# Wide source runs for the loads, and engine programs written without a block, in a batched matrix product

## The chip, the cores and the metric

The kernel runs on one core of a Trainium2 chip. The metric is the device time of one execution in microseconds (us), the median of several. The profiler also records one execution per kernel with a time stamp for every instruction, DMA packet and semaphore update; its length from the first to the last instruction is called the span, and it is about 2 us shorter than the reported time.

Engines are named as the profile names them: PE multiplies matrices (PEld loads its weights), DVE and ACT copy and cast, POOL is used here for semaphores only, SP issues the DMAs. A DMA is carried out by sixteen DMA engines, which each move a share of it and add 1 to its semaphore when their share has landed (48 DMAs leave 768 landings in the trace). HBM is the main memory, where x, y and the result lie; SBUF holds the tiles, in 128 partitions (rows); PSUM is where PE leaves its sums. A source run is a stretch of contiguous bytes that a DMA reads as one piece; a written row is a piece that it writes into one partition of SBUF.

## The reference

For each of 16 batches, x has 768 rows of 512 floats and y 768 rows of 1,024. The result is x transposed times y, 512 by 1,024.

```
batch, m, k, n = 16, 512, 768, 1024
np.einsum('bkm,bkn->bmn', x, y).astype(np.float32)
```

So 75.50 MB are read and 33.55 MB written. No order of work avoids them.

## The kernel before

Per batch, x is loaded as 128 partitions of 12,288 bytes and y as 128 of 24,576, both contiguous in HBM. DVE casts them to bf16, y in two halves, PE makes 48 matmuls of 128x512, ACT copies the sums from PSUM, and a store of 128 rows of 16,384 bytes writes the batch. Loads have two staging buffers each, outputs five; a store is issued four batches behind the loads.

```
LAG = 4
NO = 5
@block.sync
def _(sync):
    def store(b):
        sync.wait_ge(outs, b + 1)
        sync.dma_start(o_v[b], ob[b % NO][:]).then_inc(so[b % NO], 16)
    for b in range(B):
        i = b % 2
        if b >= 2:
            sync.wait_ge(cast, b - 1)            # both x and y of batch b-2 cast
        sync.dma_start(xs[i][:], x_v[b]).then_inc(sx[i], 16)
        sync.dma_start(ys[i][:], y_v[b]).then_inc(sy[i], 16)
        if b >= LAG:
            store(b - LAG)
    ...
@block.tensor
def _(tensor):
    with tensor.Fori(0, B // 2):
        batch(tensor, 0, False)
        batch(tensor, 1, False)
@block.scalar                                     # one copy for each 128x1024 of sums
...
```

## Time and profile before

| | before |
|---|---|
| median time, us | 262.99 (262.69 to 263.14) |
| span of the profiled execution, us | 261.2 |
| x: DMA issue to landing, us | 20.8 |
| y: DMA issue to landing, us | 27.7 |
| DMA queue's share of sixteen engines' span | 98.1% |

The last line is the one to start with. The prediction below shows the lines of the page and of the table by stage. The issues of the profile (what, engine, count, size, median us from issue to landing) show how deep the queue is:

```profile
ys<-in_y_dram SPq DMA_DIRECT2D x16, 3072.0 KB, 27.7
out_dram<-ob SPq DMA_DIRECT2D x16, 2048.0 KB, 32.1
xs<-in_x_dram SPq DMA_DIRECT2D x16, 1536.0 KB, 20.8
```

An x of 1.57 MB needs 3.7 us of moving. It lands 20.8 us after its issue because other transfers stand ahead of it.

### The profile page before, as it was taken

Reading aid. Unit: us, or ns where it says so; the run is one execution under the profiler, and the core shown is the slowest. Engines: PE = TensorE matmul, PEld = TensorE weight load, DVE = VectorE, ACT = ScalarE, POOL = GpSimd, SP = SyncE. Lnnn points to the kernel's source line nnn. Section 1 sums busy time; section 2 is a strip of 40 time slices with the busy share of each in tenths; the row PEclk is TensorE's granted clock in tenths of the full one; section 3 lists DMA queues with packets and bytes.
Section 4 is the critical chain, followed back from the end, with each engine's and each line's share of the span. In section 5 each row is a group of like instructions: output and inputs, shape, how many; then the busy total and the mean of one; then the engine's idle time right before and its main releaser. Section 6 shows DMA issues by size and latency. Waiting matters only on the chain. (4 is left out here: it accounts for less than half of the span.)

```text
span 261.2 us, 1938 instructions
## 1 busy us (share of the span) xinstructions
PE 188.0 (72%) x768; PEld 87.1 (33%) x768; DVE 83.0 (32%) x48; ACT 66.1 (25%) x65; POOL 0.2 (0%) x4
## 2 busy tenths in 40 slices
PE   0039999998948949398595997939678394896920
PEld 0014555443513515144152342514334142342500
DVE  0261734435223252322524214252132523225000
ACT  1003343433331314114032140412314033131410
POOL 0000000000000000000000000000000000000000
PEclk9999999999986999979798697997999899797995
DMA  7999999999999999999999999999999999999993
GB/s 265 431 425 427 438 411 453 425 386 418 446 420 439 420 430 446 415 441 420 439 437 412 447 423 440 415 432 442 423 434 420 435 433 423 440 433 421 434 421 141
DMA packets 6915, 109.09 MB, mean 418 GB/s; under 512 B 768, under 2 KB 768, under 8 KB 768
## 3 DMA queue, kind: packets, MB, share of 16 engines
q1 hardware_dynamic: 6912, 109.05, 98.1%
q8 instruction: 1, 0.02, 0.0%
q14 instruction: 2, 0.02, 0.0%
HBM read 75.50 MB, written 33.55 MB: 417 GB/s over the span
## 5 line engine op out<-in xcount | busy, mean ns | idle before, releaser
L105 PE MATMUL ps<-yb,xb 128*128 128x512 bf16 x768 | 188.0, 406 | 61.6 <-PEq L100 55.9
L105 PEld LDWEIGHTS ps<-yb,xb 128*128 128x128 bf16 x768 | 87.1, 116 | 162.1 <-issue 96.7
L125 ACT COPY ob<-ps 128x1024 f32<-128x1024 f32 x64 | 64.9, 1013 | 183.6 <-PE ps L105 183.6
L93 DVE CAST yb<-ys 128x3072 bf16<-128x3072 f32 x32 | 54.9, 1757 | 88.4 <-DMA ys<-in_y_dram 88.4
L89 DVE CAST xb<-xs 128x3072 bf16<-128x3072 f32 x16 | 28.2, 1760 | 67.5 <-DMA xs<-in_x_dram 66.8
L125 ACT ACT_TABLE_LOAD x1 | 1.3, 1283 | 1.0 <-SPq L44 1.0
L142 POOL MEMSET const-uint8-127<- 128x1 uint8 x1 | 0.1, 102 | 0.0
L142 POOL MEMSET const-bfloat16-1.0<- 128x1 bf16 x1 | 0.1, 101 | 0.0
L142 POOL MEMSET const-float32-0.0<- 128x1 f32 x1 | 0.1, 98 | 0.2 <-issue 0.2
L142 POOL MEMSET const-float32-1.0<- 128x1 f32 x1 | 0.1, 98 | 0.0
## 6 DMA issues: line engine op xcount, KB each, us to landing
ys<-in_y_dram SPq DMA_DIRECT2D x16, 3072.0 KB, 27.7
out_dram<-ob SPq DMA_DIRECT2D x16, 2048.0 KB, 32.1
xs<-in_x_dram SPq DMA_DIRECT2D x16, 1536.0 KB, 20.8
```

The costliest lines, as they stand in the source:

```text
L89: nc.vector.tensor_copy(xb[i][:], xs[i][:]).then_inc(ready, 1)
L93: nc.vector.tensor_copy(yb[i][:, ks], ys[i][:, ks]).then_inc(ready, 1)
L105: mm = nc.tensor.matmul(ps[mo][:, nt], x_w[:, kt, mo], yb[i][:, kt, nt * NF:(nt + 1) * NF], start=(kt == 0), stop=(kt == KT - 1))
L125: nc.scalar.copy(ob[b % NO][:, mo].rearrange("p (t f) -> p t f", f=NF), ps[mo][:]).then_inc(room, 1)
L142: nc = _bacc.Bacc("TRN2", target_bir_lowering=False, num_devices=1)
```

## The change

The intent: the block goes (the frame that the engines' programs stand in, with a barrier at its end, where the engines wait for each other); each staging buffer is given back as soon as its own cast is done; and source runs are made as long as they can be, 49,152 bytes, which span four partitions of x or two of y. The first load of x and of y stays plain and serves as a pattern for the others. Casts of y become one instruction in batches 3 to 13, copies from PSUM become half as many and twice as large, and POOL passes the casts' count to PE. The core of the diff (cut at "..."):

```
-    ps = [... nc.psum_tensor(f"ps{i}", [P, NT, NF], FP32) for i in range(MT)]
+    HB = MT // 2
+    ps = [... nc.psum_tensor(f"ps{i}", [P, HB, NT, NF], FP32) for i in range(2)]
...
-    block = ec(nc.Block())
...
+    def wide_dma(key, dst, src, dram_rows, load):
+        ...
+        widen = lambda a: a.rearrange("(q r) k m -> q (r k m)", r=dram_rows)
+        plain = lambda a: a.rearrange("p k m -> p (k m)")
+        s, d = (widen(src), plain(dst)) if load else (plain(src), widen(dst))
...
+        if b < B - 2:
+            nc.sync.wait_ge(groups, 2 * (b + 2))
+        else:
+            nc.sync.wait_ge(outs, b - (B - 3))
...
+        if b >= 2:
+            nc.sync.wait_ge(cast, nx[b - 2])
+        wide_dma("x", xs[i][:], x_v[b], 4, True).then_inc(sx[i], 16)
+        if b >= 2:
+            nc.sync.wait_ge(cast, nx[b - 2] + parts(b - 2))
+        wide_dma("y", ys[i][:], y_v[b], 2, True).then_inc(sy[i], 16)
...
+    for b in range(B):
+        nc.gpsimd.wait_ge(cast, nx[b]).then_inc(ready, 1)
...
```

More of the change, by code (lines that the diff above doesn't have):

```diff
@@ L3 @@
 _os.environ.setdefault("NEURON_RT_ULTRASERVER_MODE", "4")
+import copy as _copy
 from contextlib import ExitStack
@@ L10 @@
 from concourse._compat import with_exitstack
+from concourse.ordered_engine_set import OrderedEngineSet
 @with_exitstack
@@ L41 @@
     KH = KT // 2
-    GP = NT * NF
     ctx.enter_context(tc.tile_critical())
@@ L50 @@
     ob = [ec(nc.sbuf_tensor(f"ob{i}", [P, MT, N], FP32)) for i in range(NO)]
-    ps = [ec(nc.psum_tensor(f"ps{i}", [P, NT, NF], FP32)) for i in range(MT)]
+    HB = MT // 2
+    ps = [ec(nc.psum_tensor(f"ps{i}", [P, HB, NT, NF], FP32)) for i in range(2)]
     sx = [ec(nc.semaphore(f"sx{i}")) for i in range(2)]
@@ L59 @@
     outs = ec(nc.semaphore("outs"))
-    block = ec(nc.Block())
-    @block.sync
-    def _(sync):
-        def store(b):
-            sync.wait_ge(outs, b + 1)
-            sync.dma_start(o_v[b], ob[b % NO][:]).then_inc(so[b % NO], 16)
-        for b in range(B):
-            i = b % 2
-            if b >= 2:
-                sync.wait_ge(cast, b - 1)
-            sync.dma_start(xs[i][:], x_v[b]).then_inc(sx[i], 16)
-            sync.dma_start(ys[i][:], y_v[b]).then_inc(sy[i], 16)
-            if b >= LAG:
-                store(b - LAG)
-        for b in range(B - LAG, B):
-            store(b)
-        for i in range(NO):
-            sync.wait_ge(so[i], 16 * len(range(i, B, NO)))
@@ L81, in _ @@
-    @block.vector
-    def _(vector):
-        for b in range(B):
-            i = b % 2
-            n = 16 * (b // 2 + 1)
-            if b >= 2:
-                vector.wait_ge(groups, MT * (b - 1))
-            vector.wait_ge(sx[i], n)
-            nc.vector.tensor_copy(xb[i][:], xs[i][:]).then_inc(ready, 1)
-            vector.wait_ge(sy[i], n)
-            for h in range(2):
-                ks = slice(h * KH, (h + 1) * KH)
-                nc.vector.tensor_copy(yb[i][:, ks], ys[i][:, ks]).then_inc(ready, 1)
-            vector.drain().then_inc(cast, 1)
@@ L96, in batch @@
-    def batch(tensor, i, first):
-        x_w = xb[i][:].rearrange("p k (j mo) -> p k mo j", mo=MT)
-        tensor.wait_ge(ready, 2).then_inc(ready, -2)
-        for mo in range(MT):
-            tensor.wait_ge(room, 1).then_inc(room, -1)
-            for nt in range(NT):
-                for kt in range(KT):
-                    if mo == 0 and nt == 0 and kt == KH:
-                        tensor.wait_ge(ready, 1).then_inc(ready, -1)
-                    mm = nc.tensor.matmul(
-                        ps[mo][:, nt], x_w[:, kt, mo],
-                        yb[i][:, kt, nt * NF:(nt + 1) * NF],
-                        start=(kt == 0), stop=(kt == KT - 1))
-            mm.then_inc(groups, 1)
@@ L111, in _ @@
-    @block.tensor
-    def _(tensor):
-        with tensor.Fori(0, B // 2):
-            batch(tensor, 0, False)
-            batch(tensor, 1, False)
-    @block.scalar
-    def _(scalar):
-        nc.scalar.nop().then_inc(room, MT)
-        for b in range(B):
-            for mo in range(MT):
-                if mo == 0 and b >= NO:
-                    scalar.wait_ge(so[b % NO], 16 * (b // NO))
-                scalar.wait_ge(groups, MT * b + mo + 1)
-                nc.scalar.copy(ob[b % NO][:, mo].rearrange("p (t f) -> p t f", f=NF),
-                               ps[mo][:]).then_inc(room, 1)
-            scalar.drain().then_inc(outs, 1)
+    made = {}
@@ new lines, in wide_dma @@
+    def wide_dma(key, dst, src, dram_rows, load):
+        if key not in made:
+            made[key] = nc.sync.dma_start(dst, src)
+            return made[key]
+        pat = mybir.BassSymbolicTensorAccessPattern
+        widen = lambda a: a.rearrange("(q r) k m -> q (r k m)", r=dram_rows)
+        plain = lambda a: a.rearrange("p k m -> p (k m)")
+        s, d = (widen(src), plain(dst)) if load else (plain(src), widen(dst))
+        return nc.sync.add_instruction(_copy.replace(
+            made[key].ins, name=nc.get_next_instruction_name(),
+            ins=(pat(ap=s.ap, dtype=s.dtype, bass_ap=s, is_dma=False),),
+            outs=(pat(ap=d.ap, dtype=d.dtype, bass_ap=d, is_dma=False),),
+            sync_info=None, ant_dge_precooked=False))
@@ new lines, in parts, with store @@
+    def parts(b):
+        return 2 if b in (0, 1, 2, 14, 15) else 1
+    nx = [sum(1 + parts(a) for a in range(b)) + 1 for b in range(B)]
+    def store(b):
+        if b < B - 2:
+            nc.sync.wait_ge(groups, 2 * (b + 2))
+        else:
+            nc.sync.wait_ge(outs, b - (B - 3))
+        nc.sync.dma_start(o_v[b], ob[b % NO][:]).then_inc(so[b % NO], 16)
+    for b in range(B):
+        i = b % 2
+        if b >= 2:
[4 more added lines that the diff above has]
+        wide_dma("y", ys[i][:], y_v[b], 2, True).then_inc(sy[i], 16)
+        if b >= LAG:
+            store(b - LAG)
@@ new lines @@
+    for b in range(B - LAG, B):
+        store(b)
+    for b in range(B):
+        i = b % 2
+        n = 16 * (b // 2 + 1)
+        if b >= 2:
+            nc.vector.wait_ge(groups, 2 * (b - 1))
+        nc.vector.wait_ge(sx[i], n)
+        nc.vector.tensor_copy(xb[i][:], xs[i][:]).then_inc(cast, 1)
+        nc.vector.wait_ge(sy[i], n)
+        for h in range(parts(b)):
+            ks = slice(h * KT // parts(b), (h + 1) * KT // parts(b))
+            nc.vector.tensor_copy(yb[i][:, ks], ys[i][:, ks]).then_inc(cast, 1)
@@ new lines, with batch @@
+    for b in range(B):
+        nc.gpsimd.wait_ge(cast, nx[b]).then_inc(ready, 1)
+        for h in range(parts(b)):
+            nc.gpsimd.wait_ge(cast, nx[b] + h + 1).then_inc(ready, 2 // parts(b))
+    def batch(i):
+        x_w = xb[i][:].rearrange("p k (j mo) -> p k mo j", mo=MT)
+        nc.tensor.wait_ge(ready, 2).then_inc(ready, -2)
+        for g in range(2):
+            nc.tensor.wait_ge(room, 1).then_inc(room, -1)
+            for m in range(HB):
+                for nt in range(NT):
+                    for kt in range(KT):
+                        if g == 0 and m == 0 and nt == 0 and kt == KH:
+                            nc.tensor.wait_ge(ready, 1).then_inc(ready, -1)
+                        mm = nc.tensor.matmul(
+                            ps[g][:, m, nt], x_w[:, kt, g * HB + m],
+                            yb[i][:, kt, nt * NF:(nt + 1) * NF],
+                            start=(kt == 0), stop=(kt == KT - 1))
+            mm.then_inc(groups, 1)
@@ new lines @@
+    pe = nc.tensor.engine
+    with nc.Fori(0, B // 2, engines=OrderedEngineSet([pe])):
+        batch(0)
+        batch(1)
+    nc.scalar.nop().then_inc(room, 2)
+    for b in range(B):
+        if b >= NO:
+            nc.scalar.wait_ge(so[b % NO], 16 * (b // NO))
+        for g in range(2):
+            nc.scalar.wait_ge(groups, 2 * b + g + 1)
+            cp = nc.scalar.copy(ob[b % NO][:, g * HB:(g + 1) * HB].rearrange("p m (t f) -> p m t f", f=NF),
+                                ps[g][:])
+            if b < B - 1:
+                cp.then_inc(room, 1)
+        if b == B - 2:
+            nc.scalar.drain().then_inc(outs, 1)
@@ L131 @@
+    cp.then_inc(outs, 1)
+    for i in range(NO):
+        nc.sync.wait_ge(so[i], 16 * len(range(i, B, NO)))
 _INS = ['x', 'y']
```

## The prediction

> **What bounds the kernel now.** I read the page's busy shares first, then its DMA rows, then the busy table by stage, then the end in order of time, and last the packet and landing records of the trace.
>
> ```profile
> PE 188.0 (72%) x768; PEld 87.1 (33%) x768; DVE 83.0 (32%) x48; ACT 66.1 (25%) x65; POOL 0.2 (0%) x4
> ...
> DMA  7999999999999999999999999999999999999993
> ...
> DMA packets 6915, 109.09 MB, mean 418 GB/s; under 512 B 768, under 2 KB 768, under 8 KB 768
> ...
> q1 hardware_dynamic: 6912, 109.05, 98.1%
> ...
> L105 PE MATMUL ps<-yb,xb 128*128 128x512 bf16 x768 | 188.0, 406 | 61.6 <-PEq L100 55.9
> ...
> L93 DVE CAST yb<-ys 128x3072 bf16<-128x3072 f32 x32 | 54.9, 1757 | 88.4 <-DMA ys<-in_y_dram 88.4
> ```
>
> No compute engine is over 72%, while the queue's packets fill 98.1% of sixteen DMA engines' span. PE idles 61.6 us, most of it at the point where it waits for a batch's casts, and the casts wait 88.4 us for y to land. The chain runs from the loads to the casts to the matmuls. The table by stage (length, busy of PE, PEld, DVE, ACT, POOL, granted clock, DMA share, GB/s) says the same from start to end:
>
> ```profile
> 60.00:120.00 60.00, 45.93 (x192) 21.30 (x190) 20.76 (x12) 16.23 (x16) 0.00 (x0) 0.91 1.00 430
> 120.00:180.00 60.00, 45.87 (x174) 19.87 (x172) 19.00 (x11) 14.55 (x15) 0.00 (x0) 0.86 1.01 432
> 180.00:240.00 60.00, 44.77 (x184) 20.54 (x183) 20.76 (x12) 15.84 (x16) 0.00 (x0) 0.92 1.00 430
> 240.00:245.00 5.00, 5.00 (x24) 2.53 (x23) 0.00 (x0) 1.48 (x2) 0.00 (x0) 0.95 0.99 423
> 245.00:250.00 5.00, 4.67 (x22) 2.24 (x20) 0.00 (x0) 1.85 (x3) 0.00 (x0) 1.00 1.01 433
> 250.00:255.00 5.00, 0.00 (x0) 0.00 (x0) 0.00 (x0) 0.72 (x1) 0.00 (x0) 0.92 0.98 419
> 255.00:262.00 7.00, 0.00 (x0) 0.00 (x0) 0.00 (x0) 0.00 (x0) 0.00 (x0) 0.50 0.26 110
> ```
>
> DMA share is 1.00 in every long stage: the queue never runs dry. Only the ends are not full: the first packet starts 1.95 us into the span, and the last store is issued when the other stores are almost drained:
>
> ```profile
> 249.71 1.01 ACT L125 COPY ob<-ps 128x1024 f32<-128x1024 f32 x1 [1.58 <-PE ps L105]
> 250.78 0.33 SPq L66 DMA_DIRECT2D out_dram<-ob  x1
> ```
>
> The trace's semaphore landings show one more thing. The sixteen shares of one DMA do not land together: x of batch 0 lands over 1.16 us, and from about 38 us on the last engine is some 2.4, later 3.3 us behind the first. The one 16 KB instruction fetch in the span, a packet of 1.07 us at 38.0 us, comes just as the spread jumps from 1.17 to 2.37. The last store's shares land from 256.89 to 259.79, median 257.17; so the end is set by one laggard engine 2.6 us behind the median.
>
> **What the Trainium skill says.** "DMA: Bandwidth & Descriptors", section "Where 436 GB/s comes from", puts a ceiling of 435.2 GB/s (16 ports of 32 bytes at 850 MHz) on a core's DMA; the 430 to 432 GB/s of the stages agree and lie 1% under it. The same page, "Why small descriptors are slow (HBM only)", names a fixed overhead of about 3 cycles a packet. The packet records here have something like it, but larger: 12,288 bytes (x) take 460 ns in the median, 24,576 (y) 912 ns. The difference, 452 ns for 12,288 bytes, is 27.2 GB/s an engine, 435 over sixteen; what is left of either is **8 ns a packet**. "HBM Reference", section "Specifications (TRN2)", says a lone core is bounded by its engines at about 425 GB/s, not by the shared 358; this core ran over both figures.
>
> **The change, part by part.**
>
> Bytes do not change: 75.50 MB read, 33.55 written. At 435.2 GB/s they take 250.6 us. With the first packet at 1.95 us and 1.8 us from the last packet to the end of the span, that alone is 254.4 us of a 261.2 us span; the reported time is 1.8 us above the span (262.99 against 261.2). So no rearrangement of the same bytes can save more than about 6.8 us, 2.6%, and the bulk of these is not in reach.
>
> (a) Wide source runs. Each engine now takes 8 packets of every DMA: 16 x 8 = 128 of x and 128 of y. The landings of the fastest engine agree: y to next x 3.69 us = 8 x 460, x to y 7.30 us = 8 x 912, plus a 9 ns semaphore. If a packet is a source run, x has runs of 49,152 bytes, 2 for an engine, and y 4: 32 + 64 = 96 in place of 256 (first loads stay plain, which I neglect). 160 packets x 8 ns = **1.28 us** off each engine's queue, all of it on the path. If all 256 gaps vanished it would be 2.05 us. If the 8 ns belongs to the SBUF side, where there are still 128 rows, it is 0. Stores point to the load direction as its home: their landings step by 4.84 us, 604 ns a packet, against 602.4 at 27.2 GB/s; hardly any gap. They don't say which side. I take two thirds of 1.28: **0.85 us**.
>
> (b) Staging freed by each cast. x of batch b+2 is issued after x's cast, not after both y casts. In the first period that is about 9 us earlier (9.45 for 18.49 us). But the order in the queue stays x, y, store, and it is never empty: landing comes 20.8 (x) and 27.7 us (y) after issue. Gain **0**.
>
> (c) Own programs without the block. The block's exit is on the path: the last landing is noticed at 259.80, its barrier ends and the next stage begins at 260.18. That is up to 0.38 us; I take 0.3, and 0.05 for the entry. **0.35 us**.
>
> (d) Fewer, larger instructions. y is cast in one piece in batches 3 to 13, so PE starts a batch up to 1.76 us later; PE needs some 12 us of a period of 15.8, which leaves room. POOL relays the casts: the starting barrier's relay took 0.12 us from wait to release. Stores wait for PE having finished the next batch; that is about 3 us before the loads ahead of them can be issued. **0** in the middle.
>
> (e) The end. The last copy is 128x2048, at most twice 1.01 us, so the last store starts 1.0 us later after PE; with the relay 1.1, less the 1.4 us by which y of batch 15 would land earlier. The fast engines are through with their backlog then, and idle 1 us or so. The laggard still has over 2 us of backlog, and it sets the end: **0** if the laggard stays.
>
> Sum: 262.99 - 0.85 - 0.35 = 261.8. The spread can only be rerolled: the sides of it that I see (a 16 KB instruction fetch, first packets of 0.96 to 1.74 us) may shrink with other programs, worth up to 1.2 us. I subtract 0.2 for this: **261.6 us**.
>
> **Rivals.** *The transfer is bound by bytes, not packets*: the SBUF side sets the 8 ns, or the longer reads make the write side wait. Then (a) gives 0 and the time is 262.6. For it: 430 of 435 GB/s leaves little. Against: the gap is seen in loads and not in stores. *PE or the end becomes the bound*: if the engines level out, the last store's issue at about 250.5 us plus 5.5 us to land is the limit, span about 257.5, time 259.3; so this rival helps, and its later copy takes back up to 1 us of it. PE as the bound in the middle would need 16 x 15.8 us; it is 188 us busy. *Wide reads disturb the engines*: 48 KB runs mean that an engine stays on one region of HBM, and one stalled run delays four partitions. Nothing in the trace speaks for it; 3% lower load rate would cost 5 us (load packets are 177.5 us of each engine).
>
> **Range and chances.** Without (a) and with a worse spread 263.0; with all of the 2.05 us, the 0.35 and 0.8 of the laggard 259.9. That is my range. Faster by 2% means under 257.7: it needs the whole of (a) and nearly all of the laggard's 2.6 us together, 3%. Slower by 2% is 268.3: wide reads 3% slower and more, 3%.
>
> **What would show it.** Packets of the queue: fewer than 6,912, the x ones of some 1,816 ns in place of 4 x 460, if a record is a source run; their share of sixteen engines' span should stay near 98%. GB/s in the middle stages: 432 to 434 for 430 to 432. The landing of a y after its x on the fastest engine: 7.27 for 7.30 us; x after y 3.64 for 3.69. Issues of x about 9 us earlier in the first period with no change of landing. The last store issued between 250 and 251 us. From its last landing to the end of span some 1.1 us in place of 1.44. The prediction is wrong if the middle's rate falls (rival three), if the DMA share shows holes in the middle (a store or a load held by a later semaphore), or if the spread of landings at the end goes below 1 us or over 4.

## The result, and the profile after

The changed kernel took 262.83 us (262.80 to 262.97) beside 263.06 us of the kernel before in the same rounds; the ratio is 0.9994 with a 95% interval of 0.9976 to 1.0011. Beside later runs of before it was 0.9992 (0.9978 to 1.0006). The time is the same; 0.2 us of the 1.4 us that I had forecast came, if any.

The page of the changed kernel (busy of the engines, DMA packets, the queue, the issues as above):

```profile
PE 188.3 (72%) x760; PEld 88.9 (34%) x768; DVE 82.3 (32%) x37; ACT 61.1 (23%) x33; POOL 0.2 (0%) x4
...
DMA packets 4513, 109.07 MB, mean 418 GB/s; under 512 B 768, under 2 KB 768, under 8 KB 768
...
q1 hardware_dynamic: 4512, 109.05, 97.9%
...
ys<-in_y_dram SPq DMA_DIRECT2D x16, 3072.0 KB, 28.2
out_dram<-ob SPq DMA_DIRECT2D x16, 2048.0 KB, 32.6
xs<-in_x_dram SPq DMA_DIRECT2D x16, 1536.0 KB, 29.7
```

The change did what it set out to do: 4,512 packets in place of 6,912, and x issued some 9 us earlier. It bought nothing: the queue is still 97.9% full, at the same mean of 418 GB/s, and x waits 29.7 us from issue to landing in place of 20.8. The table by stage (columns as in the prediction) of the changed kernel:

```profile
60.00:120.00 60.00, 44.91 (x180) 21.07 (x181) 20.48 (x8) 13.08 (x7) 0.00 (x0) 0.89 1.01 436
120.00:180.00 60.00, 47.42 (x181) 21.51 (x182) 18.71 (x7) 14.93 (x8) 0.00 (x0) 0.86 1.00 431
180.00:240.00 60.00, 44.82 (x185) 21.14 (x186) 20.62 (x10) 14.94 (x8) 0.00 (x0) 0.92 0.99 426
```

Read such GB/s with care: a record's bytes are booked within its packet, and a packet of 49,152 bytes is long beside a stage's edge. The sum of the three stages is what can be compared: 431.0 GB/s in the mean, against 430.7 before. A better measure is the time from one landing to the next on the engine that lands first, where every transfer waits only for the one ahead of it:

| median step on the first engine, us | before | after |
|---|---|---|
| y of a batch, then x of the next (no store between) | 3.690 | 3.688 |
| x, then y | 7.312 | 7.306 |
| store, then store (the last store left out) | 4.838 | 4.838 |

The steps are equal to 6 ns where I had forecast 3.64 and 7.27 us. That is where the forecast gain was lost. The end in order of time, of the changed kernel:

```profile
249.74 1.87 ACT L161 COPY ob<-ps 128x2048 f32<-128x2048 f32 x1 [3.25 <-PE ps L143]
251.63 0.33 SPq L98 DMA_DIRECT2D out_dram<-ob  x1
```

PE's last result comes at the same time as before, to 0.03 us; the larger copy is 0.86 us longer and the last store is issued 0.85 us later. Yet its last share lands at 259.46 us, where it was 259.79.

### The profile page after: what moved, and what is told of

Its sections match the earlier page's. It is cut to its first block, busy times and chain, and to the rows that moved or that the text cites. A ratio compares the mean times of both kernels' runs of the same rounds, so it can differ in the third digit from the quotient of the medians.

```text
span 260.7 us, 1850 instructions
## 1 busy us (share of the span) xinstructions
PE 188.3 (72%) x760; PEld 88.9 (34%) x768; DVE 82.3 (32%) x37; ACT 61.1 (23%) x33; POOL 0.2 (0%) x4
## 3 DMA queue, kind: packets, MB, share of 16 engines
q1 hardware_dynamic: 4512, 109.05, 97.9%
## 5 line engine op out<-in xcount | busy, mean ns | idle before, releaser
L143 PEld LDWEIGHTS ps<-yb,xb 128*128 128x128 bf16 x768 | 88.9, 117 | 160.4 <-issue 95.0
L161 ACT COPY ob<-ps 128x2048 f32<-128x2048 f32 x32 | 59.8, 1869 | 189.6 <-PE ps L143 189.6
L124 DVE CAST yb<-ys 128x6144 bf16<-128x6144 f32 (+1 forms) x21 | 54.1, 2596 | 88.0 <-DMA ys<-in_y_dram 88.0
## 6 DMA issues: line engine op xcount, KB each, us to landing
xs<-in_x_dram SPq DMA_DIRECT2D x16, 1536.0 KB, 29.7
```

Of the source, the lines that this page charges most:

```text
L124: nc.vector.tensor_copy(yb[i][:, ks], ys[i][:, ks]).then_inc(cast, 1)
L143: mm = nc.tensor.matmul(ps[g][:, m, nt], x_w[:, kt, g * HB + m], yb[i][:, kt, nt * NF:(nt + 1) * NF], start=(kt == 0), stop=(kt == KT - 1))
L161: cp = nc.scalar.copy(ob[b % NO][:, g * HB:(g + 1) * HB].rearrange("p m (t f) -> p m t f", f=NF), ps[g][:])
```

## The experiments

Two theories were on the table. One: a load's rate is set by the rows that it writes into SBUF, so wide reads change nothing. The other: wide reads do gain, and another part of the change loses as much. After that came the questions of the end of the run.

**1. Wide reads alone, in the kernel before, twice.** The same helper as in the change, inside the block:

```
-            sync.dma_start(xs[i][:], x_v[b]).then_inc(sx[i], 16)
-            sync.dma_start(ys[i][:], y_v[b]).then_inc(sy[i], 16)
+            wide_dma(sync, "x", xs[i][:], x_v[b], 4).then_inc(sx[i], 16)
+            wide_dma(sync, "y", ys[i][:], y_v[b], 2).then_inc(sy[i], 16)
```

> The kernel before with the wide source runs and nothing else. Theory (a load's rate is set by the rows it writes into SBUF, 8 ns for each, and wide reads change nothing): ratio to before 1.000, an x lands 3.69 us after a y on the first engine and a y 7.31 us after an x, as before. Rival (wide reads gain 1.28 us of queue time, and another part of the change loses it): 0.995, steps of 3.64 and 7.27 us.

> The kernel before with wide source runs once more: its ratio was 0.9982 (0.9968 to 0.9996) with no step of the queue changed. Theory (wide reads do nothing; that was the spread between executions): 0.999 to 1.001. Rival (they do gain some 0.5 us in a place that I haven't found): 0.998 again, and below the changed kernel beside it.

Measured: 262.86 us beside 263.32 of before, ratio 0.9982 (0.9968 to 0.9996); the steps were 3.693 and 7.302 us. The second time: 263.04 us beside 262.95, ratio 0.9999 (0.9984 to 1.0014), steps 3.689 and 7.305. The first ratio alone looked like a gain of 0.5 us with nothing in the trace behind it; the repetition did not show it. Wide reads gain nothing that these runs can see.

**2. The change without wide reads.**

```
-        wide_dma("x", xs[i][:], x_v[b], 4, True).then_inc(sx[i], 16)
+        nc.sync.dma_start(xs[i][:], x_v[b]).then_inc(sx[i], 16)
```

and y likewise.

> The changed kernel with plain loads: the whole change without the wide source runs. Theory: same as the changed kernel, ratio to before about 0.999; rival (wide reads gain 1.28 us, the rest loses it): 1.004.

Measured: 262.89 us, ratio 0.9992 (0.9978 to 1.0005), with 6,912 packets again and steps of 3.684 and 7.307 us. The same as the changed kernel. Both directions agree: the source run's length is worth nothing here.

**3. Written rows cut in three; then source runs cut as well.**

```
         # e3: source runs of 16,384 bytes, SBUF rows in three pieces
-        s, d = (widen(src), plain(dst)) if load else ...
+        s = widen(src).rearrange("q (c e) -> q c e", c=3)
+        d = dst.rearrange("p (c k) m -> p c (k m)", c=3)
         # e4: both sides in pieces of 4,096 (x) and 8,192 bytes (y)
+        nc.sync.dma_start(xs[i][:], x_v[b], max_dma_last_dim=4096)...
+        nc.sync.dma_start(ys[i][:], y_v[b], max_dma_last_dim=8192)...
```

> The changed kernel, with each SBUF row of a load written as three pieces (x 4,096 bytes, y 8,192) from source runs of 16,384 bytes, in 15 of 16 batches. For each engine 32 more written rows a batch and 12 more source runs. Theory (8 ns a written row): 15 x 32 x 8 ns = 3.8 us longer than the changed kernel, about 266.7 us, with an x 128 ns and a y 128 ns longer on an engine. Rival (8 ns a source run, hidden so far): 15 x 12 x 8 = 1.4 us, 264.3. Third (neither costs, the 8 ns is something else): 262.8.

> As the run with three pieces a row, but the source runs are cut at the same places, so 48 source runs an engine and batch in place of 18. Theory (only written rows cost): the same as that run, about 266.7 us. Rival (source runs cost 8 ns too): 15 x 30 x 8 ns = 3.6 us above that run.

Measured: 266.02 us (ratio 1.0101) and 266.42 us (1.0119). The second run cuts its first batch too, which by the steps below is 0.3 us of the difference of 0.4. The queue lines of the run with cut rows, then of the run with both cut:

```profile
DMA packets 7393, 109.07 MB, mean 413 GB/s; under 512 B 768, under 2 KB 768, under 8 KB 768
...
q1 hardware_dynamic: 7392, 109.05, 98.2%
```

```profile
DMA packets 15105, 109.07 MB, mean 413 GB/s; under 512 B 768, under 2 KB 768, under 8 KB 6912
...
q1 hardware_dynamic: 15104, 109.05, 99.1%
```

Twice the packets, and the same 413 GB/s. The steps tell it without rounding:

| | rows written, an engine, x or y | source runs, an engine, x and y | y to x, us | x to y, us |
|---|---|---|---|---|
| changed kernel | 8 | 2 and 4 | 3.688 | 7.306 |
| rows cut | 24 | 6 and 12 | 3.840 | 7.453 |
| both cut | 24 | 24 and 24 | 3.826 | 7.460 |

Sixteen more written rows cost 152 and 147 ns: **9 ns a written row**. Eighteen more source runs for x and twelve more for y cost -14 and +7 ns, which is nothing. This holds for pieces of 4,096 bytes and more, and for no more source runs than written rows: more of them than rows was not tried, so a cost of a source run that hides behind that of a row is not excluded.

The time rose by 3.2 us for the cut rows, 0.6 less than expected, although 15 batches at 0.30 us make 4.5 us. In these two runs the stall with the first store (experiment 6) does not show: the step to y of batch 4 is 7.45 and 7.46 us, like any other. On the lagging engine that gives 1.4 us back; what remains is 3.1, and its last landing came 3.4 us later (262.84 for 259.46).

**4. What sets the end: a last store earlier, and later.** The first edit shares the last copy between ACT and DVE; the second puts a copy into a spare buffer ahead of the last one.

```
+            h = 1 if b == B - 1 and g == 1 else HB
+            cp = nc.scalar.copy(o_g[:, :h], ps[g][:, :h])
...
+    nc.vector.wait_ge(groups, 2 * B)
+    nc.vector.tensor_copy(ob[(B - 1) % NO][:, 3:4]..., ps[1][:, 1:2]).then_inc(tail, 1)
```

```
+            if b == B - 1 and g == 1:
+                nc.scalar.copy(junk[:], ps[g][:])
```

> The changed kernel with its last copy shared by ACT and DVE, so that the last store is issued some 0.9 us earlier, at about 250.7 us. Theory (one lagging engine, which still has a backlog then, sets the end): no change, 262.8 us, the last landing stays at 259.4 us and the median landing moves to about 257.0. Rival (the last store's issue sets the end): 0.9 us shorter, 261.9.

> The changed kernel with a second copy of 1.87 us ahead of the last one, so that the last store is issued 1.87 us later. Theory: the lagging engine has 1.66 us in hand (last landing 259.46, median 257.80), so the end moves by about 0.2 us, to 263.0. Rival (the last store's issue sets the end): 1.87 us longer, 264.7.

Measured: 262.84 us (ratio 0.9996, 0.9979 to 1.0012) for the shared copy, and 263.46 us (262.96 to 264.60; ratio 1.0020, 0.9988 to 1.0052) for the late one. With the shared copy the last store was issued 0.40 us earlier and not 0.9: DVE's part of the copy took 1.23 us, and PE ended 0.18 us later. In the profiled execution of the late one, the last store was issued at 254.31 us, 2.68 us later and not 1.87, since PE was 0.92 us later too:

```profile
239.08 11.53 PE L144 MATMUL ps<-yb,xb 128*128 128x512 bf16 x45 [0.70 <-PEq L143]
...
250.65 1.87 ACT L163 COPY junk<-ps 128x2048 f32<-128x2048 f32 x1 [3.25 <-PE ps L144]
252.41 1.87 ACT L164 COPY ob<-ps 128x2048 f32<-128x2048 f32 x1
```

Of these 0.92 us only 0.20 are a later start. The last 45 matmuls took 11.54 us in place of the 10.83 of the changed kernel, and the granted clock of PE was lower there. The piece of the changed kernel's chain, and the stage of 239 to 242 us of the changed kernel and of the late copy (the clock is the third number from the right):

```profile
238.88 10.83 PE ps L143 x45
```

```profile
239.00:242.00 3.00, 3.00 (x11) 1.17 (x11) 0.00 (x0) 0.00 (x0) 0.00 (x0) 0.70 1.01 431
239.00:242.00 3.00, 2.92 (x7) 1.02 (x8) 0.00 (x0) 0.00 (x0) 0.00 (x0) 0.51 0.98 421
```

So a part of the late issue is the clock's and not the edit's. The repetition of the changed kernel too issued its last store later, at 252.47 us, with a clock of 0.59 in that stage.

The expected 0.2 us was not what the late copy measured, but the two limits that it was to tell apart are plain in the landing records:

| | last store issued | its first landing | last landing of the store before it | its last landing |
|---|---|---|---|---|
| before | 250.78 | 256.89 | 254.96 | 259.79 |
| changed | 251.63 | 257.77 | 254.63 | 259.46 |
| copy shared | 251.23 | 257.31 | 254.63 | 259.45 |
| copy late | 254.31 | 260.43 | 254.83 | 260.55 |

The last landing is the later of two: the issue and some 6.1 us, or the lagging engine's landing of the store before and 4.83 us, the length of a store's share. In the first three rows the second holds, by 1.7 to 2.9 us; in the last row the first holds. The later of the two gives the last landing of all sixteen traces to 0.15 us. That is why neither the longer copy in the change nor its repair moved the end.

**5. What makes an engine lag: more instruction fetches.** PE's loop written out, so that PE's instructions have to be fetched for every batch:

```
-    with nc.Fori(0, B // 2, engines=OrderedEngineSet([pe])):
-        batch(0)
-        batch(1)
+    for b in range(B):
+        batch(b % 2)
```

> The changed kernel with PE's loop written out, eight times the matmul instructions to fetch. Theory (the laggard that ends the run is the DMA engine that fetched 16 KB of PE's instructions at 37.7 us and lost 1.45 us by it): five or more further such fetches; if they fall on one engine each adds about 1.4 us to its lag, so the spread of landings at the end grows to over 5 us and the time by several us; if they fall on different engines, more engines lag by 1.4 us. Rival (the fetch only coincides with the jump in the spread): spread and time stay, 3.2 us and 262.8 us.

Measured: 262.63 us, ratio 0.9991 (0.9974 to 1.0007). The queues of this run:

```profile
q1 hardware_dynamic: 4512, 109.05, 98.1%
q8 instruction: 6, 0.10, 0.2%
```

Six fetches of 16 KB, where the changed kernel has one. By the end of the changed kernel's run one engine was 3.23 us behind the first in landing, the next 1.45. Here there were six behind by 2.24 to 3.02 us, the next 1.38. They appeared one at a time: after the fetch at 118.1 us one engine went from 1 us or less to 2.15, after that at 198.9 one to 2.20, after that at 228.8 one to 2.23. So the fetch does not just coincide: each costs the engine that carries it 0.6 to 1.5 us (read from the sorted landings before and after), and nothing gives that back. The packets agree: each fetch took 0.94 to 1.10 us, and about 1 us after its start came one load packet of 2.29 to 2.38 us, where most of that size take 1.82. But they fell on different engines, the worst was no worse than before, and the end (259.18) came no later. Nor is the fetch all of the lag: of the 3.23 us in the changed kernel 0.69 were there from the first load, 1.45 came with the fetch and 0.88 with the stall of experiment 6. My expectation left both open; "one engine by several us" did not come.

**6. The stall of 55 to 58 us.** In the kernels before and after, even the engine that lands first loses 0.4 and 0.5 us there (x to y of batch 4 takes 7.69 and 7.83 us); the other traces of long rows and the usual stores have 7.52 to 7.76. These are rows of the table by stage, of before and of the changed kernel:

```profile
55.00:58.00 3.00, 3.00 (x16) 1.56 (x15) 0.00 (x0) 1.43 (x2) 0.00 (x0) 1.00 1.00 341
```

```profile
55.00:58.00 3.00, 3.00 (x16) 1.57 (x14) 0.00 (x0) 0.02 (x1) 0.00 (x0) 1.00 0.92 289
```

341 and 289 GB/s at a DMA share of 1.00 and 0.92: the packets are there, but they are slow. Three edits: stores one batch earlier in the kernel before (`LAG = 3`); in the changed kernel, a store of 512 bytes a partition ahead of all loads, on SP's queue; and the same on ACT's queue. The small store on SP's queue was also run together with the shared copy of experiment 4.

```
+    nc.vector.memset(ob[0][:, 0, 0:128], 0.0).then_inc(warm, 1)
+    nc.sync.wait_ge(warm, 1)
+    nc.sync.dma_start(o_v[0][:, 0, 0:128], ob[0][:, 0, 0:128]).then_inc(warmed, 16)
```

> The kernel before with stores starting one batch earlier. It asks what the stall of 55 to 58 us is, in which all engines lose 0.5 us and the laggard 0.6 to 0.9 more. If it comes with the first store, it moves to about 44 to 47 us; if it has to do with the time or the bytes moved, it stays. The time stays within 0.3 us of before either way; this is a look at a cost that neither kernel avoids.

> The changed kernel with a store of 512 bytes a partition issued ahead of all loads (zeros, overwritten later). All engines lose about 0.5 us and the lagging one about 1.4 us as the first store begins, at 55 to 58 us (44 to 47 us where stores began a batch earlier). If it is the first store as such that costs this, it is now paid in the start, where the engines idle anyway, the step from x to y of batch 4 is 7.30 us in place of 7.83, and the last landing is some 0.9 us earlier: about 262.0 us. If it has to do with the first long store or the mix of reading and writing, the stall stays at 55 to 58 us and the time is some 0.2 us longer, 263.0.

> The small first store together with the last copy shared by ACT and DVE: if the lagging engine ends earlier, the last store's issue is next to set the end, and this pair should be ahead of the small store alone: 261.7 us against 262.0. If the small store does nothing, 263.0, as the run with the shared copy alone plus the start's delay.

> The changed kernel with the small first store issued from ACT's queue, so that it doesn't hold up the first loads on SP's. Behind SP's queue order it removed the 0.5 us stall of 55 to 58 us, but the first x landed 1.3 us later. Theory (the stall is the first store's own and can overlap the start of the loads): x of batch 0 lands at 6.4 to 6.9 us, the stall is gone, the last landing at 258.6 to 259.2 us, time 262.0 to 262.5. Rival (the engines pay the 0.5 us or more wherever the first store comes): x of batch 0 lands a half to 1.3 us later, the time is 262.8 to 263.7.

With stores a batch earlier the stall came a batch earlier: the step from x to y of batch 3 was 7.97 us in place of 7.30. It goes with the first store. The time was not "within 0.3 us", though: 266.41 us, ratio 1.0144. One store more stands ahead of the last y, so PE ends 5.1 us later; the last store was issued at 255.86 us, and the first limit of experiment 4 set the end (262.11). That miss shows what the four batches of lag are for.

The same row of the small store on SP's queue, then on ACT's:

```profile
55.00:58.00 3.00, 3.00 (x16) 1.56 (x15) 0.68 (x1) 0.00 (x0) 0.00 (x0) 1.00 0.93 393
```

```profile
55.00:58.00 3.00, 3.00 (x16) 1.57 (x15) 0.05 (x1) 0.00 (x0) 0.00 (x0) 1.00 0.81 262
```

With the small store ahead on SP's queue the stall was gone (the step to y of batch 4 was 7.30 in place of 7.83), but the time was 263.68 us, ratio 1.0026. SP issued the first x 0.71 us later and it landed 1.30 us later. Whether these further 0.6 us are the stall, moved, or only the small store's own time, the runs do not tell. The pair with the shared copy was 264.15 us (1.0042), no better. In the trace of the small store alone the last store was issued only at 254.35 us (clock 0.50 from 239 to 245 us) and set the end; in that of the pair the lagging engine did, at 260.17 us, 0.72 later than with the shared copy alone. A part of the loss lies outside the span: reported time less span is 2.27 us for the small store and 2.55 for the pair, 2.06 for the changed kernel.

On ACT's queue the small store left the first x almost where it was (6.59 for 6.44 us on the first engine), but the stall too (7.85): 263.07 us, ratio 1.0003. So the stall goes with the first store on SP's queue, but it did not come in the two runs with cut rows, where SP's first store was the same. What makes it stays open, and putting it first gained nothing. No version here beats both kernels.

**7. The block alone.** The kernel before with its own instructions, straight in the engines' programs, without the block. The changed kernel was also run again beside experiment 1's repetition.

```
-    block = ec(nc.Block())
-    @block.sync
-    def _(sync):
+    sync, vector, scalar = nc.sync, nc.vector, nc.scalar
```

> The kernel before with exactly its instructions, waits and increments, but written straight into each engine's program, without the block. Reported time less span is 1.83 us in every run of kernels with the block and 2.06 to 2.5 us without it, so a part of what the missing barrier saves inside the span seems to be given back outside. Theory (it is the missing block): span some 0.2 us under before, time less span 2.06, time 0.0 to 0.1 us below before. Rival (it comes from the other instructions, fewer casts and copies, the relay on POOL): span some 0.2 us under before, time less span 1.83, time 0.2 us below before.

> The changed kernel once more, on the same chip and beside the same runs of before as the next one: ratio 0.999.

Measured: 262.66 us without the block, ratio 0.9993 (0.9979 to 1.0007); the changed kernel again 262.80, ratio 0.9992. The block's removal alone is as near to before as the whole change. In the kernel before, SP noted the last landing at 259.80 and the span ended 1.43 us later. Without the block that was 1.19 us, and 1.22 in the changed kernel. In these two its last landing was at 259.46 in both, 0.33 earlier than before; the repetition of the changed kernel had 259.57. The three traces with the block and stores at their usual place ended at 259.79 to 259.85. I have not found why, and that it is the block's doing is not shown: the lag of the slowest engine is made of single jumps (0.4 us at 137 us before, 0.5 at 105 us in the first run of experiment 1) that come at other places in each trace.

The rival won on the other question. Reported time less span is 1.83 us for before and 1.75 without the block, and 2.06 in the changed kernel. So 0.23 us of what the changed kernel saves in the span is lost outside it, and the block is not the reason. In the changed kernel's trace an 8 KB instruction fetch comes at 262.5 us, after the span; before, and without the block, two such fetches come within it, at 167 and 185 us. That fits, but nothing was tried that takes this fetch away, and the two runs with 2.27 and 2.55 us outside the span have a single such fetch too, so it stays open.

## Why the prediction was right or wrong

**What bounds the kernel** was right. The queue stayed at 97.9%, no engine took its place, and the middle had no holes (DMA share 0.99 to 1.01 in its stages).

**(a) Wide source runs** is the step that failed: "160 packets x 8 ns = 1.28 us off each engine's queue", of which "I take two thirds of 1.28: 0.85 us". The gain was 0: the steps between landings changed by 2 to 6 ns. A sign that the forecast had named came all the same: 437 of the 1,440 wide packets took 1,815 ns (1,816 forecast for x) and 431 took 1,829; the landings did not follow. The size of the gap was right, 8 ns forecast and 9 measured. Its owner was wrong. The forecast counted packets of the trace, and a packet is a source run: the count fell by 35%, the time by nothing. By experiment 3 the gap belongs to the row written into SBUF, of which there were 128 before and after. I had named that case ("If the 8 ns belongs to the SBUF side ... it is 0") and had no evidence for either. The stores, which I used, only said that the load direction has the gap. Before there was one source run to one written row, so the trace of before could not tell them apart; splitting the difference two to one was a guess.

**(b) Staging freed by each cast** was right at 0: x is issued 9 us earlier and waits 9 us longer.

**(c) The block** was forecast at 0.35 us. The end of the span has 0.21 us of it, the entry nothing (first DMA at 0.95 us, before at 0.94). The whole effect measured alone is a ratio of 0.9993 (0.9979 to 1.0007), which is not clear of 1.

**(d) Fewer, larger instructions** was right inside the span. Its blind spot was outside: "the reported time is 1.8 us above the span" was carried over as a constant, and it rose by 0.23 us, with the changed instructions (the run with plain loads has it too, 2.08 us) and not with the missing block.

**(e) The end** was right at 0, and experiment 4 shows its mechanism: the lagging engine hides a later last store. The issue itself was missed: it was to come "between 250 and 251 us", because y of batch 15 would land 1.4 us earlier, and it came at 251.63, 0.85 us later than before: y landed only 0.31 us earlier, and PE ended when it did before. The 5.5 us from issue to landing in the second rival were too few: the trace of before has 6.1.

**The spread**, "I subtract 0.2", had the last landing 0.33 us earlier; that the size fits is luck, since its cause is not known. Sum of what the two profiled executions show: 0 for (a), -0.21 at the end of the span, -0.33 at the last landing, +0.30 outside, so -0.24 us; their times differ by -0.23, as the medians do. A small slip: the lower end of the range, 259.9, is 259.8 by its own terms.

## What to carry to other kernels

When a queue is full, ask which count its overhead follows before you reduce a count: the packets of the loads in this trace are source runs, and here only the rows written had a price. A trace in which two counts are equal cannot say which of them costs; the experiment that makes them differ is small, so make it before the change. And at the end of a run that is bound by DMA, look at the landings of the sixteen engines apart: the last one, not the last store's issue, may set the time.

## What the Trainium skill lacked or had wrong

- "DMA: Bandwidth & Descriptors", section "Why small descriptors are slow (HBM only)", puts the fixed overhead of about 3 cycles on each packet. For these long loads the runs put 9 ns on each row written into SBUF (x to y 7.306 to 7.453 us for 16 more rows), and nothing on a source run as long as there are no more of them than rows (48 in place of 18 a batch and engine: -14 and +7 ns); stores step at 604 ns for 16,384 bytes, where the loads' slope of 27.2 GB/s would make it 602.
- "Runtime: NRT & Kernel Launch", section "Instruction fetch mechanics", says that instructions come in 16 KiB blocks, mostly hidden. The trace agrees on the size. Five more fetches did not lengthen the run (262.63 us), but the DMA engine that carries a block falls 0.6 to 1.5 us back and stays there, and the slowest one ends the run (259.46 us against a median of 257.80).
- No page has the stall that comes with the first store on SP's queue: at 55 to 58 us even the first engine loses 0.4 us before and 0.5 after, elsewhere when the store is moved (0.7 us a batch earlier), none in the two runs with SBUF rows of 8,192 bytes and less.
- "HBM Reference", section "Specifications (TRN2)", has about 425 GB/s for a lone core. Here 430.7 GB/s were held from 60 to 240 us, before the change, mixing loads and stores, 1% under the 435.2 that the prediction quotes.
